# Ragged multi-head attention on one core: the order of matmuls and evacuations in the 512-row, 480-row and two-tile halves

## The chip, the cores and the metric

The kernel runs on one core of one Trainium2 chip. The metric is the device time of one execution in microseconds; lower is better. A core has a matrix engine (PE, with its weight loads shown apart as PEld), three engines that compute on vectors (DVE, ACT, POOL), SP, which here only issues transfers, and DMA queues. Each engine runs its own program; they meet at semaphores.

## The reference

For each of 32 batches only the first `lengths[b]` of 512 rows count. They are projected to Q, K and V, eight heads of 64 columns attend to each other, and the rows behind the length are zero in the output.

```python
for b in range(batch):                      # 32
    seq_len = lengths[b]                    # 64 to 511
    qkv = x[b, :seq_len] @ w_qkv            # 512 -> 3 x 512
    q, k, v = split into 8 heads of 64
    attn = softmax(q @ k.T / 8)
    output[b, :seq_len] = attn @ v
```

The lengths are data, fixed for the measurement: the longest batches have 502, 447, 446 and 436 rows.

## The kernel before

**Pairs and classes.** The kernel sorts the batches by length on the chip and takes them in pairs. A pair's class is its longer length rounded up to a multiple of 32 (and one class of 340). With these lengths the classes are 512, 448, 384, 352, 352, 340, 320, 288, 256, 224, 224, 192, 160, 160, 128 and 96. A class of N rows has T = N/128 rounded up row tiles: one pair runs with 512 rows and one with 448 (T = 4), six with three tiles, six with two and two with one.

**Halves.** Each pair is worked in two halves, one for each of its batches. A half does two things at once: the scores, exponentials and attention of its own batch, and the Q, K and V projections of the batch that comes next (of W rows). So PE always has work that does not depend on the exponentials. The eight heads go in four pairs of heads, i = 0 to 3. A half computes scores of head pairs 1, 2 and 3 of its own batch and then those of head pair 0 of the next one, so that the next half begins with an exponential that is ready. Attention A0 to A3 multiplies the exponentials with V and divides by the sum of each row.

**Banks.** Scores go to two slots, s0 and s1 (the tensor `psc`), in turn; ACT reads a slot with the exponential and writes `ep`. Projections and attention go to banks a0 and a1 (`pa`) and v0 and v1 (`pav`). A semaphore for each bank and reader says that it is full (`f_s0_act`, `f_a0_act`, and so on); another says that it is free. A group of matmuls waits until its bank is free; DVE or ACT then evacuates it. Scores contract over 64 rows of the array, the two heads of a pair on its two halves at the same time; plain projections and attention contract over 128. A crosswise pair (E, closed by F, G, H or I) splits a projection into two contractions over 64 rows, so that Q and K run on the two halves of the array together.

**What sets the order.** `half` (L761) reads a string of tokens and records, for each class, the programs of PE, ACT and DVE. S is one block of scores, Qi and Ki are projections, Bi is Q and K of head pair i in one bank, Vt is V of row tile t, Ai is attention of head pair i, O stores the output by ACT, `+` interleaves a group's matmuls with the group before, and a small letter gives the evacuation to ACT and not to DVE. 512 and 480 use the row of `ORDER` for T = 4 (`S S Q0 +A0 S S K0 V0 ...`): all its Q, K and V are plain, and DVE evacuates them. 448 and 416 use `FOUR`, in which Q and K are crosswise. Three tiles use `ORDER[3]` or `DENSE`, two tiles `ORDER[2]`: `S S B0 b1 A0 A1 b2 S S V1 b3 A2 O A3 R3 X3 V0`.

**Stores.** The output of a batch is stored in two parts. ACT issues one of them (`act_store`, from the token O): it loads the index of the batch from memory into a register, waits until attention is written, and issues the transfer (L1527). In two-tile second halves it also issues the second part of the first half's batch, ahead of its own. SP issues the rest. `read_class` (`c`) loads the word that chooses the next pair's class. POOL casts x and masks.

## Time and profile before

| | us |
|---|---|
| median of 3 runs (lowest, highest) | 333.07 (332.78, 334.8) |
| span of the profiled execution, the one time that its profile gives | 330.1 |
| 512-row pair: first half, second half | 19.39, 18.89 |
| 448-row pair: first half | 17.59 |
| two-tile stage, twelve halves | 75.29 |
| weight loads (PEld), DVE, ACT, POOL busy in the span | 205.5, 203.6, 242.4, 68.7 |

A time in the trace counts from the start of the span. A stage begins with its first scores and ends where those of the next one begin. Rows of a timeline give the start, the duration, the engine, the source line, the operation, the tiles out<-in with their shape, and in brackets an idle time ahead of it with what ended it. `ACTq` is ACT's sequencer, which issues transfers. The profile models the ends of pipelined matmuls, so the starts of rows are compared, and not the ends.

### The profile page before, as it was taken

How to read it: one execution, taken by the hardware profiler on the slowest of the kernel's cores; microseconds unless marked ns; L12 is line 12 of the kernel's file. 1: busy time of each engine (PE TensorE's matmuls, PEld its weight loads, DVE VectorE, ACT ScalarE, POOL GpSimd, SP SyncE). 2: the span in 40 equal slices, each digit the busy share in tenths (PEclk: the TensorE clock that was granted, in tenths of full speed). 3: DMA queues.
4: the chain of work that ended last, by engine and by line, in shares of the span. 5: the costliest groups of instructions: out<-in, count | busy, mean ns of one | idle time of the engine just before them, and what ended most of it. 6: DMA issues, size and time to landing. Idle time of an engine off the chain costs nothing. (4 is left out here: it accounts for less than half of the span.)

```text
span 330.1 us, 12320 instructions
## 1 busy us (share of the span) xinstructions
PE 316.4 (96%) x4353; PEld 205.5 (62%) x4354; DVE 203.6 (62%) x587; ACT 242.4 (73%) x358; POOL 68.7 (21%) x135
## 2 busy tenths in 40 slices
PE   7899999999999999999999999999999999999880
PEld 2565445455565656656666677677777777677750
DVE  3576576656585575576476557655755566767662
ACT  4577878788889879878778887787677676566531
POOL 3452220201111201210220222022111131131331
PEclk9999999999999999999999999999999999999996
DMA  6957599987656996985997999897689979965952
GB/s 195 341 138 263 94 375 310 292 179 279 153 194 142 326 263 145 323 286 149 283 314 169 235 319 216 214 291 235 212 139 174 214 199 183 170 201 148 200 145 70
DMA packets 83289, 72.42 MB, mean 219 GB/s; under 512 B 41660, under 2 KB 64188, under 8 KB 83204
## 3 DMA queue, kind: packets, MB, share of 16 engines
q1 hardware_dynamic: 69700, 58.27, 70.0%
q10 hardware_dynamic: 13504, 13.11, 11.8%
q8 instruction: 42, 0.69, 0.8%
q14 instruction: 43, 0.35, 0.4%
HBM read 25.32 MB, written 36.70 MB: 188 GB/s over the span
## 5 line engine op out<-in xcount | busy, mean ns | idle before, releaser
L367 ACT ACTIVATE ep<-psc 128x896 f16<-128x896 f32 (+9 forms) x184 | 146.8, 847 | 44.0 <-PE psc L324 34.0
L324 PE MATMUL pa<-xT,w_r 128*128 128x160 f16 (+19 forms) x952 | 127.8, 277 | 1.2 <-PEq L62 1.2
L324 PEld LDWEIGHTS pa<-xT,w_r 128*128 128x128 f16 (+1 forms) x952 | 73.0, 97 | 29.2 <-issue 10.1
L324 PE MATMUL psc<-qkT 64*128 64x224 f16 (+17 forms) x700 | 66.7, 285 | 0.6 <-ACT ep L408 0.4
L324 PE MATMUL pa<-w_r,xT 128*128 128x512 f16 (+4 forms) x332 | 58.6, 328 | 0.3 <-DVE v_aug L560 0.3
L324 PE MATMUL pav<-xT,w_r 64*128 64x352 f16 (+12 forms) x384 | 58.3, 306 | 0.0
L440 DVE CAST qkT<-pa 128x512 f16<-128x512 f32 (+9 forms) x59 | 33.4, 566 | 40.0 <-PE pa L324 36.2
L408 ACT ACTIVATE ep<-psc 128x864 f16<-128x864 f32 (+3 forms) x56 | 49.7, 946 | 10.9 <-PE psc L324 6.5
L324 PE MATMUL pav<-v_aug,ep 128*128 128x65 f16 x1268 | 54.9, 194 | 1.7 <-PEq L62 1.7
L1968 POOL MEMSET v_aug<- 128x256 f16 x28 | 8.8, 313 | 225.5 <-POOLq L1519 225.5
L324 PEld LDWEIGHTS pav<-v_aug,ep 128*128 128x128 f16 x1268 | 48.8, 98 | 10.0 <-issue 3.0
L439 ACT CAST qkT<-pa 128x320 f16<-128x320 f32 (+8 forms) x74 | 34.2, 466 | 16.6 <-PE pa L324 10.8
L661 DVE SCALAR_TENSOR_TENSOR onat<-pav,masks,rcp 128x128 f32<-128x128 f32 (+1 forms) x120 | 41.4, 384 | 4.1 <-DVE rcp L638 1.6
L1962 POOL CAST x<-x_nat 128x1536 f16<-128x1536 f32 (+3 forms) x33 | 42.0, 1272 | 8.6 <-POOLq L1519 8.3
L324 PEld LDWEIGHTS psc<-qkT 64*128 64x128 f16 x700 | 26.7, 94 | 27.2 <-issue 16.7
L463 DVE TENSOR_TENSOR v_aug<-pa,masks 128x512 f16<-128x512 f32 (+1 forms) x46 | 30.8, 674 | 15.0 <-PE pa L324 14.4
L324 PEld LDWEIGHTS pav<-xT,w_r 64*128 64x128 f16 (+1 forms) x384 | 29.8, 95 | 11.6 <-issue 1.6
L324 PEld LDWEIGHTS pa<-w_r,xT 128*128 128x128 f16 (+2 forms) x332 | 22.9, 99 | 18.3 <-issue 4.9
L324 PE MATMUL pav<-w_r,xT 128*128 128x512 f16 (+3 forms) x132 | 24.0, 333 | 0.0
L638 DVE RECIPROCAL rcp<-pav 128x8 f32<-128x8 f32 (+2 forms) x66 | 12.9, 195 | 17.5 <-PE pav L324 14.7
L324 PEld LDWEIGHTS pa<-v_aug,ep 128*128 128x128 f16 x524 | 19.3, 98 | 6.3 <-issue 2.6
L440 DVE CAST qkT<-pav 128x352 f16<-128x352 f32 (+7 forms) x27 | 14.4, 539 | 14.1 <-PE pav L324 13.4
(99 smaller groups left out, 181.4 us busy)
## 6 DMA issues: line engine op xcount, KB each, us to landing
out_dram<-zt SPq DMA_DIRECT2D x16, 768.0 KB, 5.7
x_nat<-in_x_dram SPq DMA_DIRECT2D x12, 512.0 KB
out_dram<-onat ACTq DMA_DIRECT2D x21, 256.0 KB, 3.8
x_nat<-in_x_dram SPq DMA_DIRECT2D x5, 1024.0 KB
out_dram<-onat ACTq DMA_DIRECT2D x12, 384.0 KB, 4.8
out_dram<-onat SPq DMA_DIRECT2D x12, 384.0 KB, 4.4
x_nat<-in_x_dram SPq DMA_DIRECT2D x17, 256.0 KB, 6.5
x_nat<-in_x_dram SPq DMA_DIRECT2D x4, 768.0 KB
```

What stands on the lines that cost most here:

```text
L324: return lambda e: e.matmul(o, lhsT, rhs, start=start, stop=stop)
L367: return e.activation(out=dst[at], in_=src[at], func=AF.Exp, scale=scale)
L408: lambda e, par=par, b=b: e.activation(out=ep[:, i, par, 0:T, 0:N], in_=psc_f[:, par, 0 : T * N].rearrange("p (t n) -> p t n", n=N), func= ...
L439: return lambda e: e.copy(out=dst, in_=src)
L440: return lambda e: e.tensor_copy(out=dst, in_=src)
L463: return lambda e: e.tensor_tensor(out=v_aug[h][:, t, lo // HD : lo // HD + n, 0:HD], in0=area[b][:, 0:w].rearrange("p (a d) -> p a d", d=HD),
L638: pr.add("dve", lambda e: e.reciprocal(out=rv, in_=den).then_inc(s_r, 1))
L661: ins = e.scalar_tensor_tensor(scalar=now[0][:, 1, t : t + 1], op0=ALU.mult, op1=ALU.mult, **ops)
L1962: e.tensor_copy(out=x16[h][:, 0:T, :], in_=x_nat[h][:, 0:T, :]).then_inc(s_xc[h], 1)
L1968: e.memset(v_aug[h][:, T - 1, NPAIR:NH, 0:HD], 0.0)
```

## The change

It has three parts.

**512 and 480 rows** get a list of their own. Q and K are crosswise, one half on each of two banks: `e3:a0,v0` opens the pair for head pair 3 on banks a0 and v0, `E3dd` closes it with both evacuations on DVE (`a` is ACT). Between them stands scores block S, one at a time. V and attention are no longer interleaved: attention runs in pieces of two row tiles (`A00`, `A01`), each on one bank, in stretches of whole groups. Three copies of Q or K per half (in E1ad, E2da, E0ad) and three V evacuations (V3a, V1a, V2a) go to ACT, the latter as a Copy with the row mask as its scale (`v_out`). All four of a0, a1, v0, v1 are one tensor, `pall`.

**448, 416 and the three-tile classes** are written out as lists of the same form, with the bank beside each token in place of a queue of banks that the code turned. Their groups keep their banks; at 448 V and attention are no longer interleaved.

**Two tiles** get lists `TWO` and a function `half_two`. A half now starts with the scores of head pairs 1 and 0 of its own batch (`S1 S0`: head pair 0 is no longer computed ahead), then Q and K of the next batch's head pairs 0 and 1 crosswise (`e0 e1 E0 E1`), whose evacuations are one copy of two banks each, on DVE. Then come scores `S2 S3`, attention and V. Q and K of head pair 2 (`B2a`) and in narrow classes V of tile 0 (`V0a`) are evacuated by ACT, and head pair 3 (`B3d`) last, by DVE. The class word `c` and the store O stand at the end, behind the last evacuation on ACT. The bridge to one-tile pairs waits for v0 and v1 in place of a0.

```diff
-        4: "S S Q0 +A0 S S K0 V0 S S Q1 +A1 S S K1 V1 S S Q2 +A2 S S K2 V2 S S Q3 +A3 S S V3 K3 O",
...
-        2: "S S B0 b1 A0 A1 b2 S S V1 b3 A2 O A3 R3 X3 V0",
...
-    FOUR = "S E1 S G1 S E2 S G2 S E0 S E3 S G0 G3 S S A0 Z0 V1 +A1 S S Z1 V3 +A2 S O S V0 +Z2 S A3 Z3 S S V2"
...
+        512: "e3:a0,v0 S E3dd S e1:a1,v1 S E1ad S e2:a0,v0 S e0:a1,v1 S E2da E0ad S S A00:v0 A01:a0 R00 X00 R01 A10:a1 X01 A11:v1 S R10 X10 R11 X11 S V3a:v0 V0d:a0 S c S V1a:a1 A20:v1 A21:v0 O S S R20 X20 R21 A30:a0 X21 R30 V2a:v1 X30 S A31:a1 R31 S X31",
...
+        448: "S e1:v0,a0 S E1dd S e2:v1,a1 S c E2da S e0:v0,a0 S e3:v1,a1 S E0da E3da S S A00:v0 R00 X00 A01:a0 R01 X01 V1d:v1 A10:a1 R10 X10 S S V3d:v0 A11:a0 R11 X11 A20:v1 R20 X20 S O S V0d:a1 A21:v0 R21 X21 S A30:a0 R30 X30 A31:v1 R31 X31 S S V2d:a1",
...
+    def v_out(b, h, i, T, of, eng="dve"):
...
+        if eng == "act":
+            def scaled(e):
+                rv = e.snap(regs_act["rank"], min_val=0, max_val=B - 1)
+                return e.activation(
+                    out=v_aug[h][:, t, lo // HD : lo // HD + n, 0:HD],
+                    in_=room[b][:, 0:w].rearrange("p (a d) -> p a d", d=HD), func=AF.Copy,
+                    scale=masks[:, bass.ds(rv, 1), 0, t : t + 1].rearrange("p o t -> p (o t)"),
+                )
...
+    def two_cross(pr, h, i, bs, W, engs=None):
...
+        eng = engs[0]
+        for b in bs:
+            pr.take(eng, full[(b, eng)])
+            pr.busy[b] = bs[0]
+        pr.joined.update({bs[0]: bs[1], bs[1]: bs[0]})
+        src, dst = two_banks(bs)[:, :, 0:W], qkT[h][:, 2 * i : 2 * i + 2, 0:W]
+        pr.add(eng, lambda e: (e.copy if eng == "act" else e.tensor_copy)(
+            out=dst, in_=src).then_inc(free[bs[0]], 1))
...
+    LATE = ("v0", "v1")
+    TWO = {
+        False: "S1 S0 e0:a0,a1 e1:v0,v1 E0d E1d S2 S3 A00:a0 A01:a1 R0 X00 X01 V0d:v0 V1d:v1 A20:a0 A21:a1 R2 X20 X21 B2a:v0 c B3d:v1 O",
+        True: "S1 S0 e0:a0,a1 e1:v0,v1 E0d E1d S2 S3 V1d:a0 A00:v0 A01:v1 R0 X00 X01 B2a:s0 A20:a0 A21:a1 R2 X20 X21 V0a:v0 c B3d:v1 O",
+    }
...
+            elif k == "O":
+                if h == 1:
+                    pr.take("act", s_of[0][1])
+                    pr.add("act", lambda e: store(
+                        e, e.snap(regs_act["first"], min_val=0, max_val=B - 1), 0, 1, 2))
+                act_store(pr, h, 0, 2)
+                if h == 0:
+                    pr.add("act", lambda e: e.reg_mov(regs_act["first"], regs_act["tmp"]))
```

How the order of instructions moves is seen at three places. In the rows, `psc<-qkT` are scores, `pa<-xT,w_r` projections of Q and K, `pa<-w_r,xT` those of V, and `<-v_aug,ep` attention; a digit behind a name is the buffer.

PE before, in a 512-row half (its own batch in buffer 0, the next one in buffer 1), from the middle of a Q that is interleaved with attention:

```order
L324 MATMUL pa<-xT_1,w_r 128x512
L324 MATMUL pav<-v_aug_0,ep 128x65 x8
L324 MATMUL pa<-xT_1,w_r 128x512
L324 MATMUL pav<-v_aug_0,ep 128x65 x8
L324 MATMUL psc<-qkT_0 128x512 x4
L324 MATMUL pa<-xT_1,w_r 128x512 x4
L324 MATMUL pa<-w_r,xT_1 128x512 x4
L324 MATMUL psc<-qkT_0 128x512 x4
```

PE after, in the dense first part of the same half and into its first attention:

```order
L333 MATMUL psc<-qkT_0 128x512 x2
L333 MATMUL pa<-xT_1,w_r 128x512 x8
L333 MATMUL psc<-qkT_0 128x512 x2
L333 MATMUL pa<-xT_1,w_r 128x512 x16
L333 MATMUL psc<-qkT_0 128x512 x4
L333 MATMUL pa<-v_aug_0,ep 128x65 x64
L333 MATMUL psc<-qkT_0 128x512 x4
L333 MATMUL pa<-w_r,xT_1 128x512 x8
```

All Q and K have moved together behind single blocks of scores, as 64-row matmuls (two for each one before, over half the rows), and attention and V stand in blocks of their own.

PE before, a second half of 160 rows (own batch in buffer 1, next one in buffer 0):

```order
L324 MATMUL psc<-qkT_1 128x160 x8
L324 MATMUL pa<-xT_0,w_r 128x160 x16
L324 MATMUL pav<-v_aug_1,ep 128x65 x16
L324 MATMUL pa<-xT_0,w_r 128x160 x8
L1241 ISA
L1245 TENSOR_LOAD codes
L324 MATMUL psc<-qkT_1 128x160 x4
L324 MATMUL psc<-qkT_0 128x160 x4
L324 MATMUL pa<-w_r,xT_0 64x256 x8
L324 MATMUL pa<-xT_0,w_r 128x160 x8
L324 MATMUL pav<-v_aug_1,ep 128x65 x16
L324 MATMUL pa<-w_r,xT_0 128x512 x4
```

PE after, the same half:

```order
L333 MATMUL psc<-qkT_1 128x160 x8
L333 MATMUL pa<-xT_0,w_r 128x160 x32
L333 MATMUL psc<-qkT_1 128x160 x8
L333 MATMUL pa<-w_r,xT_0 64x256 x8
L333 MATMUL pa<-v_aug_1,ep 128x65 x16
L333 MATMUL psc<-xT_0,w_r 128x160 x8
L333 MATMUL pa<-v_aug_1,ep 128x65 x16
L333 MATMUL pa<-w_r,xT_0 128x512 x4
L1363 ISA
L1367 TENSOR_LOAD codes
L333 MATMUL pa<-xT_0,w_r 128x160 x8
```

The second block of scores now comes directly behind the crosswise projections, and the half ends with a plain projection where it ended with attention and V.

ACT before, the end of that half and the start of the next (`f_..._act` is the wait for a full bank, `s_of` for written attention, L1523 the load of the batch index):

```order
L439 CAST qkT_0<-pa 128x2x160 [waits f_a0_act]
L862 ISA [waits s_of01]
L1527 DMA out_0_dram<-onat_0 128x2x256
L1522 ISA
L1523 TENSOR_LOAD idx
L1524 ISA
L1527 ISA [waits s_of10]
L1527 DMA out_0_dram<-onat_1 128x2x256
L1384 UNCONDITIONAL_BRANCH
L367 ACTIVATE ep<-psc 128x2x2x160 [waits f_s0_act]
```

ACT after, at the same place:

```order
L448 CAST qkT_0<-psc 128x2x160 [waits f_s0_act]
L474 ISA [waits f_v0_act]
L475 ACTIVATE v_aug_0<-pa,masks 128x8x64
L861 ISA [waits s_of01]
L1649 DMA out_0_dram<-onat_0 128x2x256
L1644 ISA
L1645 TENSOR_LOAD idx
L1646 ISA
L1649 ISA [waits s_of10]
L1649 DMA out_0_dram<-onat_1 128x2x256
L1506 UNCONDITIONAL_BRANCH
L376 ACTIVATE ep<-psc 128x2x2x160 [waits f_s0_act]
```

The stores have kept their place on ACT, between its last evacuation and the next half's first exponential; that evacuation is now of V, and on PE one projection is left behind it.

## Prediction

> **What bounds the kernel now.** I read the page's busy times first, then the stretches of each stage, and then the timelines of PE and ACT at the places that the change rewrites.

> ```profile
> PE 316.4 (96%) x4353; PEld 205.5 (62%) x4354; DVE 203.6 (62%) x587; ACT 242.4 (73%) x358; POOL 68.7 (21%) x135
> ```

> ```profile
> 24.56:43.95 19.39, 19.39 (x210) 9.47 (x210) 12.42 (x28) 15.50 (x16) 4.31 (x4) 1.00 0.71 197
> ...
> 235.38:310.67 75.29, 74.96 (x1084) 56.62 (x1084) 47.93 (x128) 51.92 (x85) 17.86 (x36) 1.00 0.87 186
> 256.90:263.86 6.96, 6.96 (x89) 5.28 (x90) 3.80 (x10) 4.95 (x7) 1.54 (x3) 1.00 0.97 202
> ```

> The columns are the stretch, its length, then busy us of PE, PEld, DVE, ACT, POOL, the granted clock, and the DMA share with its GB/s. The first row is one half of 512 rows, the second the whole two-tile stage (twelve halves), the third one of its halves at 224 rows. PE has no gap in any of them: a half lasts as long as its matmuls and the changes between them. Whatever makes PE wait is paid in full, and nothing in these stages hides it.

> **The halves of 512 rows.** Matmuls over 64 rows (scores) and over 128 rows (the rest) alternate:

> ```profile
> 24.56 0.61 PE L324 MATMUL psc<-qkT 64*128 64x512 f16 x4
> 25.10 0.39 PE L324 MATMUL pa<-xT,w_r 128*128 128x512 f16 x1
> ...
> 27.59 1.04 PE L324 MATMUL pa<-xT,w_r 128*128 128x512 f16 x4
> 28.46 1.03 PE L324 MATMUL pa<-w_r,xT 128*128 128x512 f16 x4
> 29.42 0.60 PE L324 MATMUL psc<-qkT 64*128 64x512 f16 x4
> ```

> Four 128-row matmuls take 28.46 - 27.59 = 0.87 us, so 0.22 each; before scores the same four take 29.42 - 28.46 = 0.96, so going into a 64-row block costs 0.09. Four score matmuls run two at a time, 0.43 of stream, and take 25.10 - 24.56 = 0.54: coming out costs 0.11. A block costs 0.20 us. Before, a 512 half has eight blocks; now Q and K are 64-row too and join the scores, and five are left. Six blocks over the two halves save 1.2 us; the number of streamed columns stays.

> The price is on ACT, which takes three Q/K copies and three V evacuations per half:

> ```profile
> L367 ACT ACTIVATE ep<-psc 128x1024 f16<-128x1024 f32 x39 | 37.9, 1021 | 9.3 <-PE psc L324 8.8 <-ACTq L62 0.6
> ...
> L439 ACT CAST qkT<-pa 128x512 f16<-128x512 f32 x3 | 1.8, 585 | 0.9 <-PE pa L324 0.8
> ```

> No row has a V evacuation on ACT; the copy of the same 512 columns, 0.585, is the nearest, its lower bound the copy, its upper the exponential of twice the columns, 1.02. I take the copy: 15.50 + 6 x 0.585 = 19.0 us of ACT in a half of at most 19.4. With that little slack some scores will wait for a bank: I charge 0.4 a half (bounds 0 and 1.6, which would be six exponentials' length less the slack). Net -1.2 + 0.8 = -0.4 us, between -1.2 and +2.

> The 448-row and three-tile lists write the same matmuls on the same banks in the same order, but for V and attention no longer interleaved at 448: nothing on either side, and PE streams the same columns.

> **The two-tile halves**, which the diff rewrites too. Before: two scores, Q/K, attention, two scores, Q/K, V. Now: S1 S0, two crosswise Q/K pairs (e0 e1 E0 E1), S2 S3, attention, V, and last a plain Q/K. PE saves one block, 0.20 us a half. But S2 and S3 write the banks of S1 and S0, so both exponentials have to be over in the time of four crosswise groups, and ACT gets its stores immediately before them. PE at 160 rows, then ACT:

> ```profile
> 294.34 0.45 PE L324 MATMUL psc<-qkT 64*128 64x160 f16 x8
> 294.72 1.31 PE L324 MATMUL pa<-xT,w_r 128*128 128x160 f16 x16
> ...
> 297.94 0.73 PE L324 MATMUL pa<-xT,w_r 128*128 128x160 f16 x8
> 298.50 0.65 PE L324 MATMUL pav<-v_aug,ep 128*128 128x65 f16 x16
> 299.18 1.02 PE L324 MATMUL pa<-w_r,xT 128*128 128x512 f16 x4
> 300.13 0.45 PE L324 MATMUL psc<-qkT 64*128 64x160 f16 x8
> ```

> ```profile
> 291.39 0.42 ACT L439 CAST qkT<-pa 128x320 f16<-128x320 f32 x1 [0.48 <-PE pa L324]
> 291.87 1.30 ACT L367 ACTIVATE ep<-psc 128x640 f16<-128x640 f32 x2
> 293.05 0.43 ACT L439 CAST qkT<-pa 128x320 f16<-128x320 f32 x1
> 293.70 0.38 ACTq L1527 DMA_DIRECT2D out_dram<-onat  x1
> 294.69 1.30 ACT L367 ACTIVATE ep<-psc 128x640 f16<-128x640 f32 x2 [1.21 <-PE psc L324]
> ...
> 298.79 0.42 ACT L439 CAST qkT<-pa 128x320 f16<-128x320 f32 x1
> 299.04 1.48 ACTq L1527 DMA_DIRECT2D out_dram<-onat  x2
> 300.87 1.30 ACT L367 ACTIVATE ep<-psc 128x640 f16<-128x640 f32 x2 [1.66 <-PE psc L324]
> ```

> ```profile
> 292.47 0.70 ACT L367 ACTIVATE ep<-psc 128x640 f16<-128x640 f32 x1
> ```

> At a second half's end ACT issues two stores with an index load between them, and the next exponential starts 300.87 - 298.79 = 2.08 us after the last evacuation did. PE had begun the scores at 300.13, and at the first half's end an exponential follows its scores in 294.69 - (294.34 + 0.13) = 0.22 us; here it is 0.4 late. That costs nothing before, because attention and V (298.50 to 300.13, 1.6 us) stand between ACT's last evacuation and the next scores, and 2.5 us of 128-row work between the two score blocks. At a first half's end the chain is one store: 0.65 to its start, 0.38 for it, about 0.1 to go on, 1.13.

> Now only the plain Q/K stands behind the last evacuation, and the class word (291.87 - 291.39 = 0.48 from cast to exponential) moves to the same place in first halves. Let z be the start of that evacuation; its matmuls ended at z - 0.22. The walk at 160 rows after a second half:
> - plain Q/K, 8 matmuls, 298.50 - 297.94 = 0.56: z + 0.34. Into 64-row mode 0.10, S1 and S0 0.27, and four crosswise groups. Their rate:

> ```profile
> 135.34 0.76 PE L324 MATMUL pav<-xT,w_r 64*128 64x352 f16 x8
> 135.94 0.76 PE L324 MATMUL pa<-xT,w_r 64*128 64x352 f16 x8
> ```

> - eight take 0.60 at 352 columns, 0.27 at 160, four groups 1.09. S2 is due at z + 1.80.
> - exponentials start at z + 2.08, one takes 0.70, two 1.30: S2's bank is free at z + 2.78, S3's at z + 3.38. PE waits 0.98, writes S2 (0.13), waits 0.47. With 0.1 for the release, 1.55 us.

> After a first half the chain is 1.13 + 0.48 = 1.61: waits 0.51 + 0.47 + 0.1 = 1.08. Each half saves the block's 0.20 and PE's present wait for V's evacuation:

> ```profile
> 281.75 1.04 PE L324 MATMUL pa<-w_r,xT 128*128 128x512 f16 x4 [0.29 <-DVE v_aug L560]
> ```

> I take 0.2 of it (298.50 to 299.18 shows 0.68 for sixteen attention matmuls of 0.49). Net +1.15 after second halves, +0.68 after first ones. At 224 rows:

> ```profile
> 248.77 0.53 ACT L439 CAST qkT<-pa 128x448 f16<-128x448 f32 x1
> ...
> 250.91 1.73 ACT L367 ACTIVATE ep<-psc 128x896 f16<-128x896 f32 x2 [1.61 <-PE psc L324]
> ...
> 255.69 0.54 ACT L439 CAST qkT<-pa 128x448 f16<-128x448 f32 x1
> 256.62 0.39 ACTq L1527 DMA_DIRECT2D out_dram<-onat  x1
> ```

> ```profile
> 261.65 0.93 PE L324 MATMUL pa<-xT,w_r 128*128 128x224 f16 x8
> 262.42 0.65 PE L324 MATMUL pav<-v_aug,ep 128*128 128x65 f16 x16
> ```

> The chain is 2.14 after a second half; two exponentials 1.73, one 0.92; S2 is due at z - 0.22 + 0.77 + 0.10 + 0.37 + 1.53 = z + 2.55. Waits 0.51 + 0.62 + 0.1, less 0.20: +1.0. After a first half the chain is about 1.7 (0.75 between 0.65 and 256.62 - 255.69 = 0.93, 0.38, 0.1, 0.48): 0.08 + 0.62 + 0.1 - 0.20 = +0.6.

> The first two-tile half comes after a three-tile one, without that chain, and loses this gap:

> ```profile
> 235.38 0.63 PE L324 MATMUL psc<-qkT 64*128 64x256 f16 x8 [0.37 <-ACT ep L408]
> ```

> -0.37 - 0.20, plus the score unit of pair 0 that is now computed twice there, 0.21, and about 0.1 on S3's bank: -0.3. At the end the bridge to one tile waits for the same chain, about +0.5: the chain stays, while 0.43 of PE work in place of 1.0 stands ahead of the bridge's scores. The stage: -0.3, halves 2 to 5 0.6 + 1.0 + 0.6 + 1.0, halves 6 to 12 4 x 0.68 + 3 x 1.15 = 6.2, and 0.5: **+9.6 us**. DVE is next: two casts of 2 x 224 columns and a third of 448 in place of one add about 2.2 us to its 3.80 of 6.96, which the longer half covers; without the chain they would be the next thing late.

> [...]

> **Sum.** 9.6 - 0.4 = +9.2. It is made against the profiled execution, whose span is 330.1; the median of the runs is 333.07, 3.0 above, and I keep that difference: 342.3 us, +2.8%. About 1% is what a measurement here can tell from no change.

> **Rivals.**
> - The chain does not bind: ACT's sequencer gets to the stores while the evacuation still waits for PE. Exponentials then start 0.22 after their scores (z + 0.79 at 160, over at 1.49 and 2.09; S3 due at 1.93), PE waits some 0.2, nets -0.15 a half at 160 and -0.06 at 224: -1.3 - 0.3 for the stage, -0.4 at 512, 331.1. Against it: an exponential 0.4 late behind each pair of stores. Chance 0.11.
> - Faster: only the blocks count, ACT never holds a bank. -0.20 x 12, -0.2 x 7, -0.37, -1.2 at 512: 327.7. It needs the first exponential by z + 0.8 and the two done in the time of four groups, 1.1 to 1.5, where they take 1.30 to 1.73. Chance 0.09.
> - Slower still: ACT also sets the 512 halves. 19.0 us, a store's 0.4, and copies that come in the dense first part, where each 1.07 of PE (a group and scores) brings an exponential of 0.97 as two take 1.94; at its upper bound +2: 344.7. Chance 0.10.
> - The forecast has 0.70, its own range 338 to 347: the S3 waits alone, 11 x 0.5, and the waits a third larger.

> Slower by over 1% is forecast and third rival, 0.80; within 1% the first, 0.11; faster the second, 0.09. The range takes in the first rival: 330.5 to 347.5.

> **What would show it.** PE idle before S2 and S3 in each two-tile half, ended by ACT's exponentials of the scores tile: some 1.0 to 1.5 us after two stores, 0.5 to 1.1 after one; halves of 7.4 to 8.0 us at 224 (6.96 now) and 6.5 to 7.0 at 160 (5.79). A 512 half of 19.0 to 19.4. I am wrong if the exponential behind the stores starts under 1 us after the last evacuation, or if PE's waits are named DVE.

## The result, and the profile after

| | before | after |
|---|---|---|
| median of the runs, us | 333.21 (332.78 to 334.8, 4 runs) | 367.65 (364.57 to 371.21, 4 runs) |
| span of the profiled execution, us | 330.1 | 364.2 (its own time 366.05) |
| ratio of times, with its 95% interval | 1 | 1.1004 (1.0937 to 1.1071) |

The ratio leaves out the run of 371.21, which was disturbed. The forecast was 342.3, so the direction held and some three quarters of the loss was not in the sum. The page of the kernel after has PE at 89% where it was at 96%:

```profile
PE 324.4 (89%) x4609; PEld 208.6 (57%) x4610; DVE 205.3 (56%) x618; ACT 243.3 (67%) x353; POOL 68.1 (19%) x135
```

The busy time of PE has grown by 8.0 us, the span by 34.1: most of the loss is waiting. The stretches of the kernel after, by stage (512 rows, 448 rows, the three-tile classes 384 to 352, the dense ones 340 to 288, two tiles; columns as in the prediction, with the count of instructions behind each busy time). The first one begins, here and wherever this stage is compared below, with the last V that PE computes ahead of it (23.64 us after, 23.50 before), unless another start is named:

```profile
23.64:67.76 44.12, 39.09 (x500) 21.12 (x498) 21.11 (x65) 36.72 (x45) 6.60 (x7) 1.00 0.86 264
67.76:103.85 36.09, 36.09 (x489) 20.84 (x490) 21.46 (x66) 29.22 (x38) 4.58 (x6) 0.95 0.57 167
103.85:164.07 60.22, 59.23 (x831) 35.34 (x830) 35.56 (x107) 49.67 (x79) 9.45 (x15) 1.00 0.80 220
164.07:251.09 87.02, 79.74 (x1200) 54.57 (x1197) 50.97 (x168) 62.06 (x95) 13.09 (x21) 1.00 0.80 233
251.09:345.00 93.91, 80.87 (x1277) 58.78 (x1277) 56.00 (x161) 46.45 (x67) 17.30 (x36) 0.98 0.58 145
```

The difference of each stage to the same stage of before, and what the experiments below then made of it:

| stage | before | after | difference | forecast | what it came from |
|---|---|---|---|---|---|
| 512 rows | 39.34 | 44.12 | +4.78 | -0.4 | 3.3 a late jump to the next body's code, the rest other waits |
| 448 rows | 34.56 | 36.09 | +1.53 | 0 | half the clock behind that jump |
| three tiles, 384 to 352 | 58.57 | 60.22 | +1.65 | 0 | 1.0 two waits, 0.7 open |
| three tiles, 340 to 288 | 79.41 | 87.02 | +7.61 | 0 | one bank, twice in a row |
| two tiles | 75.29 | 93.91 | +18.62 | +9.6 | 10.8 the place of the store, 7.8 the rest of the list |
| one tile | 19.43 | 19.20 | -0.23 | 0 | |

The waits of PE name three of these. Who waited, for whom, us in total, how often, the longest:

```profile
PE psc L333 <- ACT ep L376: 10.0, 20, 1.2
PE pa L333 <- DVE v_aug L482: 7.4, 8, 1.4
PE pa L333 <- PEq L63: 5.0, 11, 1.1
PE psc L333 <- issue: 3.3, 1, 3.3
```

The first row is the wait that was forecast. The second, projections that wait for V's evacuation, and the fourth, a wait for nothing that the profile shows, were not. The third gathers eleven waits at semaphores whose releaser the profile does not name: 0.89 at the start of the 512 rows and 0.31 in their middle, 0.80 and 0.18 in front of crosswise groups of the three-tile classes, the others later.

**The wait at issue.** PE where the second half of 512 rows ends and the 448 rows begin:

```profile
64.07 0.38 PE L333 MATMUL psc<-qkT 64*128 64x480 f16 x2
67.76 0.36 PE L333 MATMUL psc<-qkT 64*128 64x448 f16 x2 [3.31 <-issue]
...
69.12 1.62 PE L333 MATMUL pa<-xT,w_r 64*128 64x448 f16 x8
```

PE stands still for 3.31 us, and the profile shows no semaphore that it waits for. The branch that goes from the one class's code to the next's, on the queue of PE's weight loads (count, then shortest, median and longest duration in ns, first and last start), after and then before:

```profile
L1468 PEldq COMPARE_BRANCH  x16: 63/220/3766, 23.9 to 345.5; - x16
```

```profile
L1346 PEldq COMPARE_BRANCH  x16: 63/212/645, 23.8 to 311.0; - x16
```

The one of 3,766 ns is the jump out of the 512-row body; before, the jump at that place took 346 ns. And the matmuls behind it are slow: the stretches around it show the granted clock in the third column from the end.

```profile
64.30:67.70 3.40, 0.15 (x2) 0.00 (x0) 0.78 (x4) 1.74 (x3) 0.00 (x0) 1.00 0.50 171
67.70:70.00 2.30, 2.24 (x18) 1.00 (x20) 0.00 (x0) 1.65 (x2) 1.32 (x3) 0.83 0.31 73
70.00:72.50 2.50, 2.50 (x16) 0.93 (x12) 1.16 (x2) 1.10 (x2) 0.97 (x1) 0.50 0.39 66
72.50:76.00 3.50, 3.50 (x40) 1.75 (x38) 0.62 (x1) 3.08 (x5) 0.00 (x0) 0.98 0.28 56
```

The clock is 1.00 while PE is idle and for some 1.5 us more (0.83 over the 2.30 us from 67.70 on is half speed for their last 0.8), then 0.50. With the 0.98 of the last row that makes 0.8 + 2.5 + 0.1 = 3.4 us at half speed: eight crosswise matmuls take 1.62 us where their like takes 0.93 later. Here, behind a wait of 3.31 us, the clock fell 1.5 us after work had begun again; in the run below with the store moved, whose wait at this place is 6.7 us, it fell during the wait (0.52 from 65.0 to 66.0 us, with PE idle until 68.23).

**The dense three-tile classes.** PE after, from the end of a half to the next, then DVE after, then PE before at the same seam:

```profile
177.99 1.02 PE L333 MATMUL pa<-w_r,xT 128*128 128x512 f16 x4
180.18 1.26 PE L333 MATMUL pa<-xT,w_r 128*128 128x320 f16 x8 [1.17 <-DVE v_aug L482]
```

```profile
178.64 0.87 DVE L617 SCALAR_TENSOR_TENSOR onat<-pa,masks,rcp 128x128 f32<-128x128 f32 x3
179.43 0.69 DVE L482 TENSOR_TENSOR v_aug<-pa,masks 128x512 f16<-128x512 f32 x1
```

```profile
169.39 1.02 PE L324 MATMUL pav<-w_r,xT 128*128 128x512 f16 x4
170.25 1.25 PE L324 MATMUL pa<-xT,w_r 128*128 128x320 f16 x8
```

The last V of a half and the first K of the next follow each other on PE. Before, the queue of banks had put V on `pav`, and K on `pa` began 0.86 later, without a gap. The list of after has `V0d:a0` at its end and `K2d:a0` at its start: K has to wait until DVE, which first scales three pieces of attention, has evacuated V. The words "their groups keep their banks" in the section on the change are wrong at this seam.

**The two-tile halves.** PE after, from the last projection of a second half (312.56) into the next half of 160 rows, then ACT at the same place:

```profile
312.56 0.72 PE L333 MATMUL pa<-xT,w_r 128*128 128x160 f16 x8
313.21 0.45 PE L333 MATMUL psc<-qkT 64*128 64x160 f16 x8
313.50 1.57 PE L333 MATMUL pa<-xT,w_r 64*128 64x160 f16 x32
316.21 0.31 PE L333 MATMUL psc<-qkT 64*128 64x160 f16 x4 [1.14 <-ACT ep L376]
316.81 0.31 PE L333 MATMUL psc<-qkT 64*128 64x160 f16 x4 [0.28 <-ACT ep L376]
```

```profile
312.94 0.69 ACT L475 ACTIVATE v_aug<-pa,masks 128x512 f16<-128x512 f32 x1 [1.61 <-ACTq L63]
313.18 1.91 ACTq L1649 DMA_DIRECT2D out_dram<-onat  x2
315.45 2.49 ACT L376 ACTIVATE ep<-psc 128x640 f16<-128x640 f32 x4 [1.82 <-issue]
```

This is the forecast's walk. The two stores stand behind the last evacuation, the first exponential starts 315.45 - 312.94 = 2.51 us after it, and S2 and S3 wait for their banks in turn, 1.14 and 0.28.

### The profile page after: what moved, and what is told of

The parts are those of the page before. It is cut to its first block, busy times and chain, and to the rows that moved or that the text cites. A ratio compares the mean times of both kernels' runs of the same rounds, so it can differ in the third digit from the quotient of the medians.

```text
span 364.2 us, 12963 instructions
## 1 busy us (share of the span) xinstructions
PE 324.4 (89%) x4609; PEld 208.6 (57%) x4610; DVE 205.3 (56%) x618; ACT 243.3 (67%) x353; POOL 68.1 (19%) x135
## 5 line engine op out<-in xcount | busy, mean ns | idle before, releaser
L376 ACT ACTIVATE ep<-psc 128x1024 f16<-128x1024 f32 (+9 forms) x184 | 146.7, 852 | 46.3 <-PE psc L333 22.9
L333 PE MATMUL pa<-xT,w_r 64*128 64x160 f16 (+23 forms) x1536 | 140.0, 286 | 11.1 <-DVE v_aug L482 7.4
L333 PEld LDWEIGHTS pa<-xT,w_r 64*128 64x128 f16 (+1 forms) x1536 | 83.2, 95 | 53.4 <-DVE v_aug L482 12.4
L333 PE MATMUL psc<-qkT 64*128 64x160 f16 (+17 forms) x700 | 70.6, 286 | 15.0 <-ACT ep L376 10.0
L449 DVE CAST qkT<-pa 128x352 f16<-128x352 f32 (+9 forms) x80 | 43.3, 550 | 68.5 <-PE pa L333 65.7
L333 PEld LDWEIGHTS pa<-v_aug,ep 128*128 128x128 f16 x1792 | 63.4, 98 | 18.6 <-issue 9.4
L333 PE MATMUL pa<-v_aug,ep 128*128 128x65 f16 x1792 | 70.6, 195 | 1.7 <-PEq L63 1.5
L448 ACT CAST qkT<-pa 128x288 f16<-128x288 f32 (+9 forms) x75 | 32.7, 469 | 29.8 <-ACTq L63 15.3
L617 DVE SCALAR_TENSOR_TENSOR onat<-pa,masks,rcp 128x128 f32<-128x128 f32 x136 | 41.5, 345 | 3.6 <-DVE rcp L600 1.3
L777 DVE SCALAR_TENSOR_TENSOR onat<-pa,masks,rcp 128x256 f32<-128x256 f32 x36 | 16.2, 478 | 1.8 <-DVE rcp L763 0.8
L475 ACT ACTIVATE v_aug<-pa,masks 128x512 f16<-128x512 f32 x13 | 9.0, 692 | 10.1 <-PE pa L333 5.2
```

Of the source, the lines that this page charges most:

```text
L333: return lambda e: e.matmul(o, lhsT, rhs, start=start, stop=stop)
L376: return e.activation(out=dst[at], in_=src[at], func=AF.Exp, scale=scale)
L448: return lambda e: e.copy(out=dst, in_=src)
L449: return lambda e: e.tensor_copy(out=dst, in_=src)
L617: ins = e.scalar_tensor_tensor(scalar=now[0][:, 1, t : t + 1], op0=ALU.mult, op1=ALU.mult, **ops)
L777: ins = e.scalar_tensor_tensor(out=out_, in0=num, in1=rv, scalar=now[0][:, 1, t : t + 1], op0=ALU.mult, op1=ALU.mult,)
```

## The experiments

Times of single executions stand beside runs of before on the same chip (medians 332.6 to 332.9); 29 of these lie between 330.0 and 336.5, so small differences are read from the stages, which come from the traces.

### The store ahead of V

The store O moves from the end of both lists to the place right behind the first attention's output. `N` is what O did to ACT's register that counts the batches, and stays at the end.

```diff
-        False: "S1 S0 e0:a0,a1 e1:v0,v1 E0d E1d S2 S3 A00:a0 A01:a1 R0 X00 X01 V0d:v0 V1d:v1 A20:a0 A21:a1 R2 X20 X21 B2a:v0 c B3d:v1 O",
+        False: "S1 S0 e0:a0,a1 e1:v0,v1 E0d E1d S2 S3 A00:a0 A01:a1 R0 X00 X01 O V0d:v0 V1d:v1 A20:a0 A21:a1 R2 X20 X21 B2a:v0 c B3d:v1 N",
-        True: "... R0 X00 X01 B2a:s0 A20:a0 A21:a1 R2 X20 X21 V0a:v0 c B3d:v1 O",
+        True: "... R0 X00 X01 O B2a:s0 A20:a0 A21:a1 R2 X20 X21 V0a:v0 c B3d:v1 N",
```

> The output store of a two-tile half is issued by ACT right after attention of head pairs 0 and 1, ahead of its last evacuations, in place of at the end. In the changed kernel the two-tile stage lasts 93.9 us (75.3 before), and PE waits there 9.6 us for ACT's exponentials before S2 and S3. Theory (the stores hold the first exponentials, and these hold the score banks): the exponentials then start some 0.4 us after their scores, the waits before S2 vanish and those before S3 shrink, the stage falls to 85 +/- 1.5 and the span from 364 to 355. Rival (PE's own stream got longer, crosswise matmuls at narrow widths above all, and the exponentials would be late anyway): the stage stays above 91, with the waits at the same places. What both leave: the part above 75.3 that is no wait for ACT, about 9 us.

Measured 355.85 us. PE's wait for the exponentials, and the two-tile stage with a second half of 160 rows and the last half in it:

```profile
PE psc L333 <- issue: 6.7, 1, 6.7
...
PE psc L333 <- ACT ep L376: 0.5, 2, 0.3
```

```profile
251.51:334.58 83.07, 77.78 (x1277) 57.90 (x1277) 55.96 (x161) 46.39 (x67) 17.44 (x36) 1.00 0.65 169
321.27:327.61 6.34, 6.00 (x112) 4.50 (x110) 4.22 (x14) 3.46 (x7) 1.43 (x3) 1.00 0.54 168
327.61:334.58 6.97, 5.45 (x104) 4.22 (x105) 4.48 (x14) 3.45 (x6) 1.43 (x3) 1.00 0.53 146
```

The stage goes from 93.91 to 83.07 and the wait from 10.0 to 0.5: between these two traces the place of the store, and nothing else in the edit, makes 10.8 us. Part of it is not the waits themselves: 3.4 us at half clock (331 to 335.5, the rows at the end of this document) lie in the stage of the kernel after and not in this one. Three runs below with the store at its old place have 94.44 (other bank), 93.44 (hint later) and 92.85 (slot 0), the last two at full clock throughout, so the place alone is worth some 10. (The span falls by 10.1, to 354.1: the stages ahead and behind, with a wait at issue of 6.7 us among them, take 0.7 longer.) 7.8 us of the stage stay, by PE's busy time (77.78 against 74.96 before) 2.8 of matmuls and 5.0 of waits. The first two-tile half is 0.77 longer than before's (it begins on a0 too, behind a dense half's V). The last one takes 6.97 where before's takes

```profile
305.95:310.67 4.72, 4.72 (x89) 3.97 (x88) 3.04 (x9) 3.47 (x7) 1.43 (x3) 1.00 1.15 158
```

so 2.25 more. The other ten share 4.76, unevenly: from nothing to 0.8 each. In the half from 321.27 to 327.61 scores take 0.89 us, Q and K 2.91, attention 1.11, V 1.43 by the starts of their groups on PE; in the half of before that begins at 300.13, taken in the same way, 0.76, 2.46, 1.08 and 1.52. The loss is in Q and K, and there the crosswise part takes 1.39 for what sixteen plain matmuls did in 1.25, the two plain rests 0.75 and 0.77 where they took 0.65 and 0.56.

### The store ahead of V, Q and K plain

As above, and head pairs 0 and 1 are plain projections:

```diff
-        False: "S1 S0 e0:a0,a1 e1:v0,v1 E0d E1d S2 S3 ...
+        False: "S1 S0 B0d:a0 B1d:a1 S2 S3 ...
-        True: "S1 S0 e0:a0,a1 e1:v0,v1 E0d E1d S2 S3 ...
+        True: "S1 S0 B0d:a0 B1d:a1 S2 S3 ...
```

> As the kernel with the early store, and Q and K of head pairs 0 and 1 as plain matmuls over 128 rows (B0 on a0, B1 on a1, evacuated by DVE) in place of crosswise ones. 32 crosswise matmuls of 160 columns take 1.53 us in the changed kernel where I had counted 1.09 and 16 plain ones take 1.14 before. Theory (the crosswise form does not pay at 160 columns, since a pair of it takes 0.096 us whatever its width below some 220 columns): each of the halves of 160 rows gains 0.2 to 0.4 us over the early store, those of 224 rows nothing; stage 1 to 2 us lower. Rival (what is saved there is waited for in front of S2, whose exponentials take 1.3 us, and 0.2 us for going in and out of a 64-row block comes on top): stage the same within 0.7 us, or longer.

Measured 356.66 us; the stage takes 86.17, but a jump of 2.80 us at 291.2 and matmuls at half clock behind it (0.98 over the stage) lie in it, so the stage decides nothing. The four halves of 160 rows away from it take 6.31, 6.25, 7.14 and 6.04; in the run before they took 6.33, 6.58, 6.61 and 6.34 (before the change 5.79 to 5.82). Together that is the same within 0.2 us: three gain up to 0.3, and one loses 0.5, in which PE waits 0.59 ahead of a V for a semaphore whose releaser the profile does not name. The crosswise form is not what the stage lost most by. Nor does its time stay the same below 220 columns, as the expectation's theory has it: in the run before, 32 such matmuls take, from their start to the next group's, 1.54 to 1.64 us at 224 columns, 1.48 to 1.58 at 192, 1.16 to 1.41 at 160 and 1.13 at 128.

### Another bank for the last V of the dense lists

```diff
-        320: "K2d:a0 Q2a:a1 D ... A30:v0 R30 X30 V0d:a0",
+        320: "K2d:a0 Q2a:a1 D ... A30:v0 R30 X30 V0d:v1",
```

and the same at 340 and 288.

> The dense three-tile halves (340, 320, 288 rows) end with V of tile 0 on bank v1 in place of a0, the bank with which the next half begins. In the changed kernel PE waits 0.3 to 1.35 us there eight times, 7.4 us in all, named DVE's V evacuation, and the dense stage lasts 84.5 us (76.9 before). Theory (the fixed banks put the first projection of a half on the bank whose evacuation is the last on DVE): the waits vanish, the dense stage falls to 77 to 78 and the span by 6 to 7 us, less up to 0.7 at the first two-tile half. Rival (DVE is simply late at the end of these halves): the wait moves to the crosswise group that takes v1 next, and the stage falls by less than 3.

Measured 360.40 us. The wait of the projections for V's evacuation, and the dense stage:

```profile
PE pa L333 <- DVE v_aug L482: 0.6, 2, 0.3
```

```profile
164.30:244.32 80.02, 78.97 (x1200) 55.60 (x1196) 50.50 (x168) 62.13 (x95) 13.09 (x21) 1.00 0.88 241
```

87.02 becomes 80.02, 0.6 above before. That one bank's name in three lists cost 7.0 us is shown. (The span falls by 5.6 only, to 358.6, since the wait at issue is 5.5 us here.)

### The hint to the code, later

The jump is hinted at the first group of projections of the second half; here at the ninth, some 10 us later.

```diff
-                body.run_part(e, body.second[name], None, ahead)
+                body.run_part(e, body.second[name], None, ahead, nth=8 if T == 4 else 0)
```

> In the four-tile bodies PE's hint of the branch that leaves for the next class stands behind the ninth projection group (V3 at 512 rows) in place of the first one; nothing else moves. In the changed kernel PE stands still for 3.3 us at the end of the 512-row pair, for nothing that the profile names, and two groups after it run at half speed (1.5 us): 4.9 us. Theory (PE's code for the 448-row pair is not there: the hint now stands some 480 instruction slots ahead of its branch where it stood some 350 before, and what it fetched is lost): the stall and the slow groups vanish, the span falls by 4 to 5 us. Rival (the hint's place has nothing to do with it: a transfer or the code of the next block is late): the stall stays within 0.5 us.

Measured 364.18 us. The jump takes 3,836 ns and PE waits 3.5 us, as without the edit. When the hint is given, 18 or 8 us ahead of the jump, makes no difference here; that theory fell.

### The body at another slot

The kernel aligns its code to blocks of 256 instructions (`FETCH = 256`, with `addr_align`), and a body is laid so that its second half begins at a chosen slot of a block: slot 20 for the four-tile bodies. Counted in the program, the second half of the new 512-row body takes 501 slots (two for each of its 240 matmuls, a weight load and a multiplication, and 21 for waits and the like) where the old took 428 (208 matmuls). From slot 20 it runs to 521, beyond two blocks.

```diff
-SECOND = {4: 20, 3: AGAIN, 2: 0, 1: 0}
+SECOND = {4: 0, 3: AGAIN, 2: 0, 1: 0}
```

> The changed kernel with one number changed: PE's second-half bodies of 512 and 480 rows start at slot 0 of a block of 256 instruction slots, not at slot 20. The body takes 501 slots now (428 before); from slot 20 its end and the branch behind it lie beyond two blocks (521), from slot 0 within them (501). The late hint left the stall where it was: the branch to the 448-row code took 3.8 us with the hint 18 us ahead of it and with the hint 8 us ahead, and 3.8 to 7.4 in kernels that changed nothing there; before it took 0.35. Theory (the spill into a third block is what loses the code that the hint fetched): the branch takes under 0.5 us, no idle time of PE ahead of the first scores of 448 rows, the span falls by 3.5 to 5. Rival (the body is simply too long, or the transfer of code is late): the branch still takes over 3 us.

Measured 360.64 us. The jumps, and the 512- and 448-row stages:

```profile
L1468 PEldq COMPARE_BRANCH  x16: 63/214/522, 23.0 to 338.2; - x16
```

```profile
22.66:63.72 41.06, 38.93 (x501) 21.05 (x498) 21.11 (x65) 35.65 (x44) 6.60 (x7) 1.00 0.88 268
63.72:98.09 34.37, 34.37 (x488) 20.37 (x489) 21.46 (x66) 29.85 (x39) 4.58 (x6) 1.00 0.65 193
```

No jump is late, PE has no wait at issue, the clock stays at 1.00, and the two stages are 44.12 + 36.09 - 41.06 - 34.37 = 4.8 us shorter together. The 512 rows still take 1.7 more than before, with waits of 0.86 at the start, 0.30 in the middle and, where the late jump was, 0.88 for ACT's exponential.

### The old body at a slot from which it runs over

Before, unchanged but for the slot: 428 from 90 is 518.

```diff
-SECOND = {4: 20, 3: AGAIN, 2: 0, 1: 0}
+SECOND = {4: 90, 3: AGAIN, 2: 0, 1: 0}
```

> The kernel before, with the same number moved the other way: its second-half bodies of 512 and 480 rows (428 slots) start at slot 90, so that their last 6 slots and the branch lie in a third block. Nothing else moves, and its matmuls and their order are those of before. Theory (the spill): the branch to the 448-row code takes 3 to 7 us where it took 0.35, with half-speed matmuls behind it, and the span goes from 330 to 334 to 338. Rival (the new lists themselves, by their length or order, make the code late): no stall, the span stays within 0.7 us.

Measured 337.09 us (span 335.0). PE at the seam, and the jumps:

```profile
65.24 0.36 PE L324 MATMUL psc<-qkT 64*128 64x448 f16 x2 [3.04 <-issue]
```

```profile
L1346 PEldq COMPARE_BRANCH  x16: 63/218/4626, 23.1 to 316.3; - x16
```

The kernel before gets the same late jump and the same half clock (0.95 over the 448 rows) from the slot alone; its two stages take 42.44 and 36.07, 4.6 us more. So the late jump goes with a body that runs beyond two blocks. In all the runs of this document, the jump out of the 512-row body takes 0.35 to 0.44 us in the eight whose body ends within 512 slots and 3.8 to 7.4 in the six where it does not. The page of the kernel after has 43 packets, 0.70 MB in all, on one of its instruction queues, 16 KB each. The view of the transfers shows one of them at the jump: in the kernel after, in the stretch of the late jump, 63.93 to 67.70 us, it has

```profile
q8 instruction: 1, 0.02, 1.7%
```

one packet of 16 KB, whose transfer begins at 65.2, 2.5 us before the jump ends. The other five late jumps out of this body have one packet each too, begun 2.3 to 2.8 us before their ends; the eight jumps on time have none. What the jump waits for ahead of that, 1.0 to 4.9 us from its start to the packet's, no view tells, and why the end of the second block matters no run shows.

### The 512- and 480-row lists alone

Before, with the new lists of 512 and 480 rows and nothing else of the change, at slot 0:

```diff
+        if N > FOUR_ROWS:
+            half_list(...)
...
-SECOND = {4: 20, 3: AGAIN, 2: 0, 1: 0}
+SECOND = {4: 0, 3: AGAIN, 2: 0, 1: 0}
```

> The kernel before with the new lists of 512 and 480 rows alone (crosswise Q and K, evacuations on ACT, attention in stretches), second-half bodies from slot 0; 448 rows, three, two and one tile as before. Theory (fewer 64-row blocks, six in the pair at 0.2 us, are worth what I had counted, 1.2, and ACT's six more evacuations cost little): from the end of the prologue to the first scores of 448 rows 38.0 us (39.4 before; 38.0 to 38.3 in three kernels with the new lists when their stall and waits are taken off), span and median 1 to 1.5 us lower, 0.4%. Rival (ACT sets these halves, or PE waits at their start for the transposed x): nothing gained, 39.4 or more.

Measured 333.65 us (12 runs) against 332.64 (17 runs): 0.9992 (0.9956 to 1.0028), no difference. The 512-row stage of this kernel, from its own first matmul to the first scores of the 448 rows, then that of before:

```profile
24.50:62.76 38.26, 37.63 (x480) 20.13 (x481) 19.72 (x62) 35.62 (x44) 6.61 (x7) 1.00 0.94 263
```

```profile
24.56:62.84 38.28, 38.28 (x416) 19.09 (x416) 24.90 (x61) 30.75 (x32) 6.60 (x7) 1.00 0.92 255
```

PE is busy 0.65 us less, which may be the gain of fewer changes between 64 and 128 rows, and gives it back in a wait at the end (ahead of the stretch it waits 0.36 more, at a semaphore whose releaser is not named):

```profile
62.76 0.36 PE L325 MATMUL psc<-qkT 64*128 64x448 f16 x2 [0.62 <-ACT ep L368]
```

The 39.4 us of before in this expectation and in the next ones have the last V ahead of the stage in them, 1.1 us; the 38.0 and 38.6 beside them have not. From the end of that V on, before takes 38.28 and this kernel 38.62.

### Three tries at those waits

On that kernel, a block of scores first in the list and not last, so that a half begins with scores that are ready:

```diff
-        512: "e3:a0,v0 S E3dd S ... S A31:a1 R31 S X31",
+        512: "S e3:a0,v0 S E3dd S ... S A31:a1 R31 X31",
```

> The kernel before with the new 512 and 480 lists alone, and in these lists the first block of scores moved from the end to the start of a half (S e3 ... in place of e3 S ... S). The lists alone went from the prologue's end to the first scores of 448 rows in 38.6 us (39.4 before), with two waits left in it: 0.36 at the start, where PE needs the next batch's transposed x with its first instruction, and 0.62 at the end, where ACT is late. Theory (the list's start and end cost these waits, and a block of scores at the start covers both): 37.7 to 38.0, another 0.6 to 0.9 saved. Rival (ACT, which is busy nearly all of these halves with 19 us in 19, is the bound, and the order of the scores can't change that): 38.4 or more.

All evacuations of the list on DVE:

```diff
-        512: "... E1ad ... E2da E0ad ... V3a:v0 ... V1a:a1 ... V2a:v1 ...
+        512: "... E1dd ... E2dd E0dd ... V3d:v0 ... V1d:a1 ... V2d:v1 ...
```

> The kernel before with the new 512 and 480 lists alone, all evacuations in them by DVE (six per half move back from ACT). Theory (ACT's six evacuations, 0.58 each for Q and K and 0.70 for V, make ACT the bound and cost what the saved 64-row blocks would bring): the wait of 0.62 for ACT at the end goes, 37.9 to 38.2. Rival (DVE, in bursts of two copies of 0.69 per 2.2 us and with the normalisation behind them, is late instead): 38.6 or more, with waits that name DVE.

And both at once:

> Both together: scores first and all evacuations on DVE. Six 64-row blocks fewer at 0.2 us make 1.2 us, so from 39.4 it can come to 38.2, and to about 37.8 with the half-microsecond that the single blocks of scores between crosswise groups save besides. Theory that both waits were real: 37.7 to 38.0, the median 1.2 to 1.6 us below that of before, 0.4%. Rival (it is all covered already): 38.6, no difference.

Measured, against 29 runs of before (332.9): 0.9969 (0.9933 to 1.0004), 1.0017 (0.9983 to 1.0052) and 1.0012 (0.9975 to 1.0049). From their own first matmul the 512-row stages take 39.22, 39.91 and 38.67, against 38.28 before. Neither move frees anything: with all evacuations on DVE PE still waits 0.53 and 0.25 for ACT. That the exponentials themselves then hold the scores, one of 0.97 us for each 1.07 of PE, is not shown: with both moves at once no wait for ACT is left in the stage, and it is no shorter than before. Nor is the 0.65 firm, since the same matmuls keep PE busy for 37.90, 38.35 and 38.19 us in these three. None of them beats before.

### All four mends together

The store ahead of V, plain Q and K, the other bank and slot 0:

```diff
-SECOND = {4: 20, 3: AGAIN, 2: 0, 1: 0}
+SECOND = {4: 0, 3: AGAIN, 2: 0, 1: 0}
...
-        320: "... V0d:a0",
+        320: "... V0d:v1",
...
-        False: "S1 S0 e0:a0,a1 e1:v0,v1 E0d E1d S2 S3 ... B3d:v1 O",
+        False: "S1 S0 B0d:a0 B1d:a1 S2 S3 A00:a0 A01:a1 R0 X00 X01 O ... B3d:v1 N",
```

> The changed kernel with the store early, plain Q and K in the two-tile halves, V of tile 0 on v1 in the dense ones, and slot 0. If the three causes (stores, bank, spill) and their sizes are right and add up: stages 38 (prologue's end to 448 rows), 34.7, 60, 80, 82, 19.4, span 337 to 339, so some 7 above before: of that 6 to 7 in the two-tile stage, from its order itself. Rival (something else is paid in all stages): over 342.

Measured 342.87 us, span 341.1: 23 of the 34 us of the span are back. 512 and 448 rows take 39.75 and 34.37, within half a microsecond of before, the dense classes 80.09. What is left is 1.0 in the sparse three-tile classes (384 to 352 rows) and, above all, the two-tile stage:

```profile
237.01:320.91 83.90, 77.96 (x1085) 57.29 (x1085) 56.90 (x161) 46.72 (x67) 17.86 (x36) 1.00 0.65 174
```

8.6 more than before, 3.0 of it busy PE, the rest waits; a jump of 2.25 us at 292.24, for which PE waits 1.65, is among them.

### V last in the two-tile lists

On that kernel Q and K of head pair 3 go ahead of the second attention, on a score bank, so that V stands at the end as it did before:

```diff
-        False: "... O V0d:v0 V1d:v1 A20:a0 A21:a1 R2 X20 X21 B2a:v0 c B3d:v1 N",
+        False: "... O V0d:v0 B3d:s1 A20:a0 A21:a1 R2 X20 X21 B2a:v0 c V1d:v1 N",
-        True: "... O B2a:s0 A20:a0 A21:a1 R2 X20 X21 V0a:v0 c B3d:v1 N",
+        True: "... O B2a:s0 B3d:s1 A20:a0 A21:a1 R2 X20 X21 V0a:v0 c N",
```

> The mended kernel (store early, plain Q and K, bank, slot) with the two-tile lists' last projection of Q and K (B3) moved ahead of the second attention pair, to score bank s1, so that a half ends with V as it did before the change. The mended kernel's two-tile stage lasts 83.9 us, 2.2 of it a late branch at 292 us. Theory (what is left is the order's own: the last evacuations of a half stand bare ahead of the next half's scores, some 0.2 us in each half and 1.0 at the bridge to one tile, which needs the last Q and K): stage 80 to 81.5 without a late branch, and no wait over 0.5 us at the bridge. Rival (it is PE's stream that is longer, by the scores in two blocks of four and more changes of bank): 82 or more.

Measured 349.83 us, the stage 92.03. PE at two changes of class and at the bridge to one tile:

```profile
284.75 0.50 PE L333 MATMUL psc<-qkT 64*128 64x192 f16 x8 [3.02 <-issue]
...
302.07 0.45 PE L333 MATMUL psc<-qkT 64*128 64x160 f16 x8 [3.72 <-issue]
...
329.17 0.40 PE L333 MATMUL psc<-qkT 64*128 64x128 f16 x8 [0.87 <-PEq L63]
```

6.7 us are two late jumps, and behind each the clock is at 0.50 for a time (0.96 over the stage). The halves of 160 rows free of them take 6.42 and 6.07, where the mended kernel has 7.11 and 6.03 at the same places, but the four widest halves take 0.3 to 0.5 more each than there, so nothing is gained in all. The bridge waits 0.87 as it did (0.97 with the store moved alone): by the program it waits for banks v0 and v1, whatever was put there last. What stands last in the list is not what most of the rest of this stage is lost by.

## Why the prediction was wrong

- **Two-tile halves: the store's mechanism right, size short (+9.6 forecast, +18.6 measured).** PE's waits are named ACT's exponentials, they stand before S2 and S3, and they go when the store moves. The terms: the store chain at 312.94 is 2.51 us and not 2.08, since the two stores take 1.91 us to issue there where they took 1.48; their start, 0.24 behind the evacuation's, is as before (299.04 - 298.79 = 0.25), and behind another second half, at 328.48, they take 1.47. The waits were smaller than forecast: 0.79 to 1.61 behind second halves and 0.36 to 0.89 behind first ones, where 1.55 and 1.08 were taken at 160 rows and 1.23 and 0.80 at 224. They come to 9.6 us in this stage where the forecast's add up to 13.0; that 9.6 is also the forecast's net is chance. The forecast's 0.1 for a release and 0.1 behind a first half's store were the author's estimates; the trace after shows 0.06 (316.21 - 315.45 - 0.70) and 0.11 to 0.34. What failed is the other side of the sum, -3.4 forecast and +9.0 measured: the step "each half saves the block's 0.20 and PE's present wait". No half got shorter by it; without the chain the list still costs 7.8 us more than the old one, 2.25 of them in the last half and at the bridge, where +0.5 had stood, and 0.77 in the first, where -0.3 had stood. Before the change PE waited 0.33 us in the whole stage, so there was next to no present wait to save. Part of the loss is the rate: 32 crosswise matmuls at 160 columns, carried over from 352 columns as 1.09 us, take 1.16 to 1.41 where PE does not wait.
- **Three-tile lists: "nothing on either side" was wrong (+9.3).** The step failed at "the same matmuls on the same banks": inside a half they are, at the seam of two dense halves they are not, and that seam costs 7.0 us. A queue of banks turns on across the seam; a fixed list begins anew. Of the +1.65 of the sparse classes 0.98 are two waits in front of crosswise groups, 0.80 and 0.18, which come to 0.36 in the mended kernel; the other 0.7 is busy PE (59.23 and 59.24 where before has 58.53) and open.
- **512 rows: the forecast of -0.4 between -1.2 and +2 holds for the lists themselves.** Alone they change nothing that can be measured. Of the 1.2 us of saved changes between 64 and 128 rows, PE's busy time shows 0.65 in one trace and between -0.1 and 0.4 in the three others with these matmuls, and waits take it back. V's evacuation on ACT took 0.692 and not the copy's 0.585:

```profile
L475 ACT ACTIVATE v_aug<-pa,masks 128x512 f16<-128x512 f32 x13 | 9.0, 692 | 10.1 <-PE pa L333 5.2 <-ACTq L63 5.0
```

- **What no step had: code.** 64 more instructions for the crosswise matmuls of a second half, with some waits, push its end beyond two blocks; 6.3 us in the two four-tile stages, 4.8 of which go with the slot. The diff doubles matmuls, and the prediction counted their columns and not their instructions.
- **The rivals.** None came true. "The chain does not bind" and "only the blocks count" fell with the 10.0 us of waits; "slower still" had the right side and the wrong place: ACT does not set the 512 halves. "What would make the prediction wrong" looked for DVE behind the two-tile scores, and DVE came as the name of the wait in the dense lists.
- **The first rival's condition** was that ACT's sequencer gets to the stores while the evacuation still waits. The stores after start 313.18 - 312.94 = 0.24 us after the last evacuation has begun, not ahead of it. But that does not tell against the condition: the wait for the bank is an instruction of its own on ACT (`L474 ISA [waits f_v0_act]` in the order above), and the evacuation's row names `ACTq L63`, a wait of ACT's sequencer, so there is no waiting evacuation for the stores to pass.

Still open: the last 4.8 of the two-tile stage's 7.8 us, beyond the first half and the last one with the bridge; 0.7 of the sparse classes; and why late jumps of 1.0 to 3.9 us appear at changes of two-tile classes in some runs and not in before, whose longest is 0.645. They do not go with the new two-tile list: the kernel before with the 512-row lists alone has one, and with the body at slot 90 one of 1.0.

```profile
L1550 PEldq COMPARE_BRANCH  x16: 63/214/1622, 23.4 to 312.3; - x16
```

## What to carry to other kernels

Where an order is turned into fixed lists, read the seams as well as the lists: the last bank of one pass and the first of the next, and what one engine's last evacuation and its stores hold up in the next pass. Count a change's instructions and not only its work, since the body that ran to slot 521 here, where it had run to 448, took 3.8 us and not 0.35 at its exit, and the stage behind it lost 1.5 us at a clock of 0.95. And move a store away from the place where the next exponential is waited for: here the place alone was worth some 10 us.

## What the runs showed of the hardware that was not expected

```profile
L1473 PEldq COMPARE_BRANCH  x16: 63/209/7361, 22.8 to 335.1; - x16
```

  Giving the hint ahead of it 10 us later made no difference. Each of the late ones ended 2.3 to 2.8 us after a 16 KB packet on an instruction queue had begun.
- The clock fell to 0.50 some 1.5 us after PE had begun again, for 3.4 us, so that a wait of 3.3 us cost some 1.5 more in the next stage. It fell once more without a wait of that length, late in the two-tile stage of the kernel after, behind waits of 1.12 and 0.28; waits of 1.14 and 0.28 one pair of halves earlier (316 us) had no such fall behind them, and what made the difference is open:

```profile
331.00:333.00 2.00, 1.53 (x16) 0.77 (x16) 0.00 (x0) 1.92 (x4) 0.00 (x0) 0.76 0.86 245
333.00:335.50 2.50, 2.50 (x37) 2.49 (x36) 1.88 (x6) 0.32 (x1) 0.00 (x0) 0.51 0.27 102
```
